# Hybrid DeltaNet and dilated-attention layer: first output factor turned before the step-48 scores, single blendings and stores moved by a third of a step, row splits and last loads re-placed

## The chip, the cores and the metric

The kernel runs on one core of one Trainium2 chip. The metric is the device time of one execution in microseconds, taken as the median over runs. Engines are named as in the profile: PE (TensorE), DVE (VectorE), ACT (ScalarE), POOL (GpSimd), SP (SyncE, which here only issues DMAs; ACT issues some too).

## The reference, cut to what matters

One layer on x of 2048 x 1024 float32. A combined projection feeds two mixers whose outputs are concatenated and projected back.

```python
h = rms_norm(x, norm_w)
proj = h @ w_in                                   # 1024 x 4104
qkv_dn, z_dn, b_dn, a_dn, qkv_att, gate_att = split(proj)
y_dn  = rms_norm(gated_delta_rule(silu(conv(qkv_dn)), ...)) * silu(z_dn)   # 2048 x 512
# attention, 8 heads of 64; q and k are RMS-normed
for window, dilation in ((128, 1), (512, 4), (2048, 16)):
    scores = q k^T + rel_bias, masked to the band; lse = logsumexp(scores)
    o = softmax(scores) v
o = sum over patterns of softmax(lse) * o
y_att = o * silu(gate_att)                                                  # 2048 x 512
out = x + concat(y_dn, y_att) @ w_out             # 1024 x 1024
```

## The kernel before, in words

Up to about 800 us it projects and runs the delta rule, whose result goes to DRAM as y_d. The rest, from line 838 on, is issued exactly in the order in which the Python code stands: a `Queue` class (line 99, which is why most rows show L99) ties every instruction of an engine to the one before it.

**Attention.** Pairs of heads are worked in 8 groups G[0] to G[7], each in 12 steps, so 96 steps; `step(t, gen, n)` issues one. A step runs what the table `at_step(t, third, ...)` has put at its three thirds and these parts: scores (PE `sc` into two PSUM buffers, DVE adds the bias and takes the minimum, `pr<-sc,bias`, shown as CUSTOM_DVE_ANT_0 in the profile and ISA in the order, then ACT's exponential `pr<-pr,ml`), on odd steps the values of two earlier steps (PE `pv`, ACT copy `op`), and the turning of the scores before (PE transposes `pt`, copied to `pT` by DVE and ACT). POOL spreads queries (`qz<-q`) and copies keys (`C<-K`).

**Fill.** Between these parts PE gets matmuls of another matrix product, `n` of them in the three thirds of a step: up to step 47 the attention projections (`pj`, 128x256; a norm needs the sums `ss`, which POOL finishes by an add and a power, and DVE then writes `t<-pj,ss` and so frees the `pj` buffer), from step 48 on the output projection (`po`, 128x512). The output projection is a list of jobs, one for 128 rows and one kind of factor: "dn" (from y_d, loaded as `yt`, turned by four PE transposes `po<-cs,yt`) or "att" (from mx_d, loaded as `mt`, no turning). `split` makes two parts of a factor, ACT's CAST `mh<-po` or `mh<-mt` and DVE's subtraction `mh<-po,mh`; the job's 24 or 18 matmuls follow, three for each 128 columns (high by high weights, high by low, low by high), so the third needs DVE's part. Step 48 took 1, 1 and 4 of the generator's items, of which the first two set up weights and the first factor; later steps take 4, 4 and 3 matmuls.

**After a group's scores.** Its softmax sums go out (`ml<-mr`) and back (`mm<-ml`, six loads, `sums_back` twice with three), are weighed on DVE (`M`, `e`, `lt`), written as F, and the group is blended in four quarters `qd`: `blend_load` (Fb, gt), `blend` (POOL, ending in `gt<-gt,Fb`), and `mixed` (the store mx_d<-gt), from which att jobs load.

**Weights.** The raw rows 4 to 7 of w_out are loaded during the first jobs (`raw_load`) and split by `wo_split` at the (job, matmul) pairs in `raws`: ACT `xh<-res` or `xh<-K`, DVE `xl<-res,xh`.

**Loads.** All loads here come from SP in written order. `load(upto)` issues the loads of the factors up to a job number; `yt` and `mt` have two buffers each, so a load waits until the factor two earlier is consumed. Buffers named `bias` (two, of another pool) hold the score biases and are not used after the last group's scores.

Of the kernel before, what the change touches and what calls it, by code (L numbers as in the profile page):

```python
# [8 lines left out]
F32 = mybir.dt.float32  # L9
# [7 lines left out]
P = 128  # L17
# [67 lines left out]
def hybrid(tc, xT, x, norm_w, w_in, conv_w, a_log, dt_bias, dn_norm_w, q_norm_w, k_norm_w,  # L85
# [23 lines left out]
    nc = tc.nc  # L109
# [13 lines left out]
    dma = nc.sync.dma_start  # L123
    adma = nc.scalar.dma_start
# [94 lines left out]
    nc = engines  # L219
    dma = nc.sync.dma_start  # L220
    adma = nc.scalar.dma_start
# [4 lines left out]
    for _ in range(14):  # L226
# [5 lines left out]
                                                        bufs=3 if b + g < 2 else 1) for n in ("wh", "wl"))  # L232
# [117 lines left out]
    for g, (tb, b, i) in enumerate(groups):  # L350
# [12 lines left out]
        k = g if tb == 0 else (g - 4) % 8  # L363
# [867 lines left out]
    def take(gen, n):  # L1231
        for _ in range(n):
            next(gen, None)
# [27 lines left out]
    def at_step(t, where, f, *args):  # L1261
        todo.setdefault((t, where), []).append((f, args))
# [3 lines left out]
    for i, g in enumerate(G):  # L1266
        b = 12 * i
        if i:
            at_step(*((b - 4, 1) if i < 4 else (b - 3, 0) if i == 4 else (b - 3, 2)), g["load"])
        at_step(b - (2 if i else 3), 1, g["queries"], 0)  # L1270
        for k in range(1, 6):
            at_step(b + 2 * k - 3, 0, g["queries"], k)
        at_step(b, 0, g["keys"], 1)
        at_step(b + 4, 0, g["keys"], 2)
        for j, t, where in (((0, -1, 0), (2, 1, 0), (4, 3, 0), (5, 4, 0), (6, 6, 0), (7, 7, 2), (8, 8, 0), (10, 10, 0))
                            if i < 4 else
                            ((0, 0, 0), (2, 1, 2), (4, 3, 2), (5, 4, 0), (6, 6, 0), (7, 7, 2), (8, 8, 0), (9, 9, 2),
                             (10, 10, 0), (11, 11, 2))):
            at_step(b + t, where, g["vload"], j)
        at_step(b + 12, 1, g["sums"])  # L1280
        at_step(b + 12, 2, g["sums_out"])
        if i < 7:
            at_step(b + 13, 2, g["sums_back"], 0, dma)
            at_step(b + 14, 0, g["sums_back"], 1, dma)
            at_step(b + 15, 1, g["weigh"])
            at_step(b + 15, 2, g["weigh2"])
            at_step(b + 16, 0, g["factors"])
            for qd in range(4):
                d = i < 6
                at_step(b + 16 + qd + d, 0 if d else 2, g["blend_load"], qd)  # L1290
                at_step(b + 17 + qd + d, 0 if d else 1, g["blend"], qd, nc.gpsimd)
                at_step(b + 19 + qd + d, 0 if d else 1, g["mixed"], qd)
                at_step(b + 20 + qd + 2 * d - (i == 6), 0 if i < 6 else 2, ready.add, (i // 4, i % 4, qd))
        else:
            at_step(b + 13, 0, g["sums_back"], 0, dma)
            at_step(b + 13, 1, g["sums_back"], 1, dma)

    def run(t, where):
        for f, args in todo.pop((t, where), ()):
# [2 lines left out]
    def step(t, gen, n):  # L1302
        run(t, 0)
        if 0 <= t < NST:
            G[t // 12]["scores"](t % 12)
        take(gen, n[0])
        run(t, 1)
        if t % 2 and 0 <= t - 3 < NST:
            G[(t - 3) // 12]["values"]((t - 3) % 12)
        if 0 <= t - 1 < NST:  # L1310
            G[(t - 1) // 12]["turned"]((t - 1) % 12)
        take(gen, n[1])
        run(t, 2)
        take(gen, n[2])
# [29 lines left out]
    def half_load(tt, kind, n):  # L1344
        if kind == "dn":
            t = wo.tile([P, 512], F32, name="yt", bufs=2)
            dma(t, y_d[tt * P:(tt + 1) * P, :])
        else:
            t = wo.tile([P, 512], F32, name="mt", bufs=2).rearrange("p (k c) -> p k c", k=4)
            dma(t[:, :n], mx_d[:n, :, tt * P:(tt + 1) * P].rearrange("k p c -> p k c"))  # L1350
        return t

# [30 lines left out]
    def out_fill():  # L1383
# [15 lines left out]
        def load(upto):  # L1399
            while n_loaded[0] <= min(upto, len(jobs) - 1):  # L1400
                tt, kind, n = jobs[n_loaded[0]][:3]
                if kind == "att" and not all((tt // 8, k, tt % 8 // 2) in ready for k in range(n)):
                    return
                loaded[n_loaded[0]] = half_load(tt, kind, n)
                n_loaded[0] += 1
# [20 lines left out]
        wo_tiles(1)  # L1426
        yield
        ops = split(0)
        load(2)
        yield  # L1430
        raws = {(0, 1): (raw_load, 0), (0, 2): (raw_load, 1), (0, 12): (raw_load, 2), (0, 22): (raw_load, 3)}
        for k, at_ in enumerate(((0, 20), (1, 8), (1, 20), (2, 8))):
            raws[at_] = (lambda k=k: wo_split(4 + k, RAW[k]),)
        store = None
        nth = -1
        for i, (tt, kind, n, mm, buf) in enumerate(jobs):
            if mm is None:
                continue
            nth += 1
            first, last = mm  # L1440
            todo_ = []
            while i + 1 + len(todo_) < len(jobs):
                todo_.append(i + 1 + len(todo_))
                if jobs[todo_[-1]][3]:
                    break
            if first:
                res = RES[tt] if kind == "att" else res_load(tt, x)
                po = [None, None]
            m = 0
            for b in range(2):  # L1450
                if first:
                    po[b] = psX.tile([P, 512], F32, name="po", bufs=3)
                for _ in products(po[b], ops, b, first, last):
                    m += 1
                    if (nth, m) in raws:
                        f, *args = raws.pop((nth, m))
                        f(*args)
                    if m >= 3 * n and m % 3 == 0 and todo_:
                        nxt = split(todo_.pop(0))
                    if nth in (18, 19, 20, 21, 23) and m == 3 * n + 8:  # L1460
                        k = min(nth - 18, 4)
                        RES[Q2[k]] = res_load(Q2[k], acc_d, K0[:, k * D:(k + 1) * D] if k < 2 else None)
                    if m >= 4:
                        load(i + 3 if nth < 24 else i + 5)
                    if m == 3 * n + 4 and store:
                        dma(*store)
                        store = None
                    yield
                if last:
                    cs_ = slice(b * 512, (b + 1) * 512)  # L1470
                    nc.vector.tensor_tensor(res[:, cs_], po[b], res[:, cs_], op=ALU.add)
            assert not todo_
            ops = nxt
            if last and not (kind == "att" and n == 3):
                store = ((out if kind == "att" else acc_d)[tt * P:(tt + 1) * P, :], res)

    gen = out_fill()
    q1 = {}
    RES = {}
    for t in range(48, NST + 2):  # L1480
        if t >= 92:
            psS[:] = [psT, "pt", 2]
        step(t, gen, {48: (1, 1, 4)}.get(t, (4, 4, 3)))
    g = G[7]
    take(gen, 18)
    g["weigh"]()
# [66 lines left out]
```

## Time and profile before

| | |
|---|---|
| median of 3 runs | 1397.85 us (1396.52 to 1399.55) |
| profiled execution, its own time | 1397.04 us |
| span of its profile | 1395.2 us |
| PE busy | 1362.5 us, 98% |
| PE weight loads | 1216.4 us, 87% |
| DVE, ACT, POOL busy | 855.7, 677.6, 486.2 us (61%, 49%, 35%) |
| granted PE clock, mean | 0.997 of full |

Busy times are sums over engines that work at once. A matmul's end is modelled, so the busy time of PE overlaps between neighbours; the start of one row against the start of the row before is the safer reading. The brackets in a timeline row give the idle time just before it and the engine whose signal ended it.

### The profile page before, as it was taken

How to read it: one execution, taken by the hardware profiler on the slowest of the kernel's cores; microseconds unless marked ns; L12 is line 12 of the kernel's file. 1: busy time of each engine (PE TensorE's matmuls, PEld its weight loads, DVE VectorE, ACT ScalarE, POOL GpSimd, SP SyncE). 2: the span in 40 equal slices, each digit the busy share in tenths (PEclk: the TensorE clock that was granted, in tenths of full speed). 3: DMA queues.
4: the chain of work that ended last, by engine and by line, in shares of the span. 5: the costliest groups of instructions: out<-in, count | busy, mean ns of one | idle time of the engine just before them, and what ended most of it. 6: DMA issues, size and time to landing. Idle time of an engine off the chain costs nothing.

```text
span 1395.2 us, 28823 instructions
## 1 busy us (share of the span) xinstructions
PE 1362.5 (98%) x10262; PEld 1216.4 (87%) x10262; DVE 855.7 (61%) x2724; ACT 677.6 (49%) x1930; POOL 486.2 (35%) x572
## 2 busy tenths in 40 slices
PE   8999999999999999999999899999999999999998
PEld 7998787778888789999999889999998788888877
DVE  7535667799742358777787564635454746556464
ACT  5644425572321334444444476666556555555520
POOL 3000000000752113442343523575757385654500
PEclk9999999999999999999999999999999999999999
DMA  6654536756547736557553455273647685665764
GB/s 189 184 109 85 109 69 143 159 125 118 102 105 136 201 96 153 158 155 185 138 151 83 103 135 138 69 196 98 161 129 220 177 266 144 211 176 166 204 187 145
DMA packets 301323, 205.01 MB, mean 147 GB/s; under 512 B 149323, under 2 KB 271067, under 8 KB 300668
## 3 DMA queue, kind: packets, MB, share of 16 engines
q1 hardware_dynamic: 231372, 171.11, 49.6%
q10 hardware_dynamic: 69808, 32.06, 8.4%
q8 instruction: 81, 1.33, 0.4%
q14 instruction: 62, 0.51, 0.1%
HBM read 142.61 MB, written 60.50 MB: 146 GB/s over the span
## 4 chain that ended last, share of the span: by engine, by line
PE 80%; DVE 7%; DMA 4%; ACT 3%; POOL 2%; issue 2%; SPq 1%; ACTq 0%; DVEq 0%; POOLq 0%
PE pj L99 16%; PE po L99 10%; PE pj L207 7%; PE pj L208 7%; PE pj L206 7%; PE sc L99 7%; PE pz L99 6%; PE pv L99 4%; PE pt L99 4%; PE SU L733 2%; PE C L727 2%; ACT pr L99 1%; POOL Fb L99 1%; PE A L665 1%; PE pm L99 1%
## 5 line engine op out<-in xcount | busy, mean ns | idle before, releaser
L99 ACT ACTIVATE pr<-pr,ml 128x192 f32<-128x192 f32 (+2 forms) x384 | 156.8, 410 | 160.8 <-DVE ml L99 155.9
L99 PE MATMUL pj<-wh,xh 128*128 128x256 f32 (+1 forms) x776 | 227.1, 293 | 3.6 <-DVE t L99 2.3
L99 PE MATMUL pj<-wh,xl 128*128 128x256 f32 (+1 forms) x776 | 224.6, 289 | 0.0
L99 PE MATMUL pj<-wl,xh 128*128 128x256 f32 (+1 forms) x776 | 224.3, 289 | 0.0
L208 PE MATMUL pj<-xh,wl 128*128 128x512 f32 x512 | 203.5, 397 | 0.7 <-DVE wl L192 0.7
L206 PE MATMUL pj<-xh,wh 128*128 128x512 f32 x512 | 202.6, 396 | 0.0
L207 PE MATMUL pj<-xl,wh 128*128 128x512 f32 x512 | 202.6, 396 | 0.0
L99 PE MATMUL po<-xh,mh 128*128 128x512 f32 x424 | 148.5, 413 | 5.3 <-ACT mh L99 4.2
L99 PEld LDWEIGHTS pj<-wh,xh 128*128 128x128 f32 x776 | 146.4, 189 | 5.0 <-DVE t L99 2.7
L99 DVE CUSTOM_DVE_ANT_0 pr<-sc,bias 128x192 f32<-128x192 f32 (+2 forms) x384 | 100.1, 308 | 77.6 <-PE sc L99 76.7
L99 PEld LDWEIGHTS pj<-wh,xl 128*128 128x128 f32 x776 | 146.5, 189 | 0.5 <-issue 0.3
L99 PEld LDWEIGHTS pj<-wl,xh 128*128 128x128 f32 x776 | 146.6, 189 | 0.1
L478 DVE SCALAR_TENSOR_TENSOR cy<-cu,cw,cy 128x512 f32<-128x512 f32 x144 | 112.1, 778 | 19.8 <-ACT cy L476 17.8
L208 PEld LDWEIGHTS pj<-xh,wl 128*128 128x128 f32 x512 | 96.2, 188 | 23.4 <-DVE wl L192 1.1
L207 PEld LDWEIGHTS pj<-xl,wh 128*128 128x128 f32 x512 | 96.2, 188 | 22.1
L206 PEld LDWEIGHTS pj<-xh,wh 128*128 128x128 f32 x512 | 96.3, 188 | 21.7
L99 POOL COPY qz<-q 64x512 f32<-64x512 f32 x96 | 95.8, 998 | 54.0 <-PE sc L99 43.9
L99 DVE COPY pT<-pt 64x128 f32<-64x128 f32 (+2 forms) x220 | 69.4, 323 | 62.6 <-PE pt L99 59.1
L99 PEld LDWEIGHTS po<-xh,mh 128*128 128x128 f32 x424 | 78.0, 189 | 19.4 <-ACT mh L99 4.8
L99 POOL TENSOR_TENSOR Fb<-Fb,op 128x256 f32<-128x256 f32 x84 | 71.6, 866 | 60.1 <-DMA Fb<-F 59.5
L543 POOL MEMSET inv<- 128x1024 f32 x1 | 1.0, 955 | 260.0 <-ACT wh L191 260.0
L99 PE MATMUL po<-xl,mh 128*128 128x512 f32 x212 | 86.9, 410 | 0.0
(369 smaller groups left out, 3066.3 us busy)
## 6 DMA issues: line engine op xcount, KB each, us to landing
wraw<-in_w_in SPq DMA_DIRECT2D x44, 512.0 KB, 7.2
cv<-cy ACTq DMA_DIRECT2D x48, 256.0 KB, 2.6
Fb<-F SPq DMA_DIRECT2D x64, 192.0 KB, 5.6
xr<-in_xT SPq DMA_DIRECT2D x32, 256.0 KB, 4.0
kT<-cv SPq DMA_DIRECT2D x32, 256.0 KB, 3.5
qk<-qs ACTq DMA_DIRECT2D x64, 128.0 KB, 4.0
res<-in_x SPq DMA_DIRECT2D x13, 512.0 KB, 5.5
V<-v_d SPq DMA_DIRECT2D x20, 256.0 KB, 4.1
```

Of the source, the lines that this page charges most:

```text
L99: i = f(*args, **kw)
L206: nc.tensor.matmul(ps, wh[:, k, c * P:(c + 1) * P], xh[tb][:, kt, :], start=kt == 0, stop=False)
L207: nc.tensor.matmul(ps, wh[:, k, c * P:(c + 1) * P], xl[tb][:, kt, :], start=False, stop=False)
L208: nc.tensor.matmul(ps, wl[:, k, c * P:(c + 1) * P], xh[tb][:, kt, :], start=False, stop=kt == KT - 1)
L478: nc.vector.scalar_tensor_tensor(y, u[:, i:i + 512], cw[:, ct, i:i + 1], y, op0=ALU.mult, op1=ALU.add)
L543: eng.memset(Tt, 0.0)
L665: nc.tensor.matmul(pq[:, u], kT[:, u].rearrange("p s i -> p (s i)"), qT[:, u].rearrange("p s i -> p (s i)"), start=True, stop=True)
L727: nc.tensor.matmul(pc[:, s_], g["WQ"][:, u, s_], S0[:, s_], start=True, stop=True)
L733: nc.tensor.matmul(su[:, s_], g["Ks"][:, u, s_], VN, start=True, stop=True)
```

## The change

Seven edits to the order; no arithmetic changes.

```diff
         at_step table, groups i < 6
-                at_step(b + 17 + qd + d, 0 if d else 1, g["blend"], qd, nc.gpsimd)
-                at_step(b + 19 + qd + d, 0 if d else 1, g["mixed"], qd)
+                    k = 3 * (b + 18 + qd) + (i == 1 and qd == 3)
+                    m = 3 * (b + 20 + qd) + 3 * (i == 2 and qd == 3)
+                    at_step(*divmod(k - 3, 3), g["blend_load"], qd)
+                    at_step(*divmod(k, 3), g["blend"], qd, nc.gpsimd)
+                    at_step(*divmod(m, 3), g["mixed"], qd)
         last group
-            at_step(b + 13, 1, g["sums_back"], 1, dma)
+            at_step(b + 13, 1, g["sums_back"], 1, adma)
 half_load
-            t = wo.tile([P, 512], F32, name="mt", bufs=2).rearrange("p (k c) -> p k c", k=4)
+            if tt in (8, 13):
+                t = at0.tile([P, 3, 192], F32, name="bias", bufs=2).rearrange("p a b -> p (a b)")[:, :512]
+            else:
+                t = wo.tile([P, 512], F32, name="mt", bufs=2)
+            t = t.rearrange("p (k c) -> p k c", k=4)
 out_fill
         ops = split(0)
-        load(2)
-        for k, at_ in enumerate(((0, 20), (1, 8), (1, 20), (2, 8))):
+        for k, at_ in enumerate(((0, 20), (1, 18), (2, 10), (3, 2))):
             raws[at_] = (lambda k=k: wo_split(4 + k, RAW[k]),)
-                        load(i + 3 if nth < 24 else i + 5)
+                        load(i + (2 if nth < 4 and m < 16 else 3 if nth < 20 else 4 if nth < 24 else 5))
 main
+    take(gen, 2)
     for t in range(48, NST + 2):
-        step(t, gen, {48: (1, 1, 4)}.get(t, (4, 4, 3)))
+        step(t, gen, (4, 3, 3) if 84 <= t < 91 else (4, 4, 3))
```

In words: (1) the last quarter's blending of group 1, with its load, is a third of a step later; on POOL this puts the add and the power on `ss` ahead of that blending, which is the only change of POOL's order. (2) The last mixed store of group 2 is a step later, on SP behind the first two `yt` loads. (3) The first factor is set up before step 48, whose thirds then hold 11 matmuls instead of 4; steps 84 to 90 hold 10 instead of 11, so the matmul counts agree again from step 91 on. (4) Factor loads look ahead two jobs at first, then 3, 4 and 5, where it was 3 and 5. (5) The row splits of w_out come after 20, 42, 58 and 74 matmuls instead of 20, 32, 44 and 56. (6) The `mt` tiles of row blocks 8 and 13 take the `bias` buffers, so the later `mt` loads wait for an earlier consumer. (7) Three of the last group's six `mm` loads are issued by ACT instead of SP.

The first place is the boundary at step 48, on PE (`pj` is the last projection fill, `sc` the scores of step 48, `po<-xh` and `po<-xl` the first output job). Before:

```order
L99 MATMUL pj<-wl,xh_9197 128x256
L99 MATMUL pj<-wh,xl_9198 128x256
L99 MATMUL sc<-K_8200,qz_8743 128x192 x4
L99 MATMUL po<-cs,ml 96x128
L99 MATMUL pt<-cs,pr 128x128 x2
L99 MATMUL po<-cs,yt 128x128 x4
L99 MATMUL po<-xh_12395,mh 128x512
```

And now:

```order
L99 MATMUL pj<-wl,xh_9197 128x256
L99 MATMUL pj<-wh,xl_9198 128x256
L99 MATMUL po<-cs,yt 128x128 x4
L99 MATMUL sc<-K_8200,qz_8743 128x192 x4
L99 MATMUL po<-xh_12395,mh 128x512
L99 MATMUL po<-xl_12396,mh 128x512
L99 MATMUL po<-xh_12395,mh 128x512 x2
L99 MATMUL po<-cs,ml 96x128
L99 MATMUL pt<-cs,pr 128x128 x2
```

The four transposes moved ahead of the scores, and four matmuls of the first job stand between the scores and the next turning. On ACT at the same place the CAST of that factor stood behind the exponentials of step 48:

```order
L99 ACTIVATE t_12640<-pj,rstd 128x256 x2
L99 DMA v_d<-t_12640 128x2x256
L99 ACTIVATE pr,ml<-pr,ml 128x192 x4
L99 COPY pT_8751<-pt 64x128 x2
L99 CAST mh<-po 128x512
```

and now stands ahead of them:

```order
L99 ACTIVATE t_12639<-pj,rstd 128x256 x2
L99 DMA v_d<-t_12639 128x2x256
L99 CAST mh<-po 128x512
L99 ACTIVATE pr,ml<-pr,ml 128x192 x4
L99 COPY pT_8751<-pt 64x128 x2
```

Only the CAST moved (DVE's subtraction moved likewise, ahead of its four `pr` of step 48).

The second place is DVE around the weighing of group 3, which ends with the bias-and-minimum rows (ISA) of step 52. Before:

```order
L99 TENSOR_TENSOR xl_12682<-res,xh_12681 128x1024
L99 TENSOR_TENSOR lt<-e,mm 32x64
L99 TENSOR_TENSOR lp<-e,mm 32x64
...
L99 RECIPROCAL lt<-lt 32x64
L99 TENSOR_TENSOR e<-e,lt 32x192
L99 TENSOR_TENSOR mh<-po,mh 128x512
L99 TENSOR_TENSOR res<-po,res 128x512
L99 ISA pr,ml<-sc,bias 128x192
```

And now:

```order
L99 TENSOR_TENSOR lt<-e,mm 32x64
L99 TENSOR_TENSOR lp<-e,mm 32x64
...
L99 RECIPROCAL lt<-lt 32x64
L99 TENSOR_TENSOR e<-e,lt 32x192
L99 TENSOR_TENSOR xl_12662<-res,xh_12661 128x1024
L99 ISA pr,ml<-sc,bias 128x192
```

The row split now follows the weighing, and the factor's subtraction and the residual's addition are no longer between it and the ISA rows.

The third place is ACT in the last group, where the two-part casts of the last att factors stand (`mh<-mt` twice for row blocks 14 and 15, `C<-mt` for block 9, `mh<-bias` for block 13). Before:

```order
L99 CAST K_15654<-mt 128x384
L99 CAST mh<-mt 128x384
L99 COPY op_15665<-pv 128x512
L99 CAST C_15790<-mt 128x384
L99 CAST mh<-mt 128x384
L99 ACTIVATE e<-e 32x192
```

And now:

```order
L99 CAST K_15656<-mt 128x384
L99 CAST mh<-bias 128x384
L99 DMA mm<-ml_94 16x2x64
L99 DMA mm<-ml_94 16x8x16
L99 DMA mm<-ml_94 16x32x4
L99 COPY op_15667<-pv 128x512
L99 CAST C_15792<-mt 128x384
L99 CAST mh<-mt 128x384
L99 ACTIVATE e<-e 32x192
```

Three DMA issues were added to ACT's order ahead of the last `op` copy and two casts; on SP the same three are gone, and the loads of blocks 9 and 14 now go out together ahead of `ml<-mr`, where 13 and 9 did.

## Rows read from the trace of the kernel before

**Rows 1.** The page, part 1: busy us of each engine, share of the span, instructions.

```profile
PE 1362.5 (98%) x10262; PEld 1216.4 (87%) x10262; DVE 855.7 (61%) x2724; ACT 677.6 (49%) x1930; POOL 486.2 (35%) x572
```

**Rows 2.** Table of windows: start:end and length, busy us of each engine with its instructions, granted PE clock, DMA share, GB/s.

```profile
1066.00:1077.00 11.00, 7.97 (x38) 6.75 (x37) 6.09 (x22) 6.14 (x22) 4.84 (x4) 0.84 0.71 223
1116.00:1329.00 213.00, 213.00 (x1670) 184.01 (x1669) 118.25 (x495) 122.27 (x462) 127.54 (x133) 1.00 0.68 197
```

**Rows 3.** Waits of PE from 838 us to the end: who waited for whom, us in total, times, longest.

```profile
PE po L99 <- ACT mh L99: 4.2, 2, 2.5
PE pj L99 <- DVE t L99: 2.3, 1, 2.3
PE pt L99 <- ACT pT L99: 1.8, 1, 1.8
```

**Rows 4.** Timelines of POOL, DVE and PE, 983 to 993 us: start, duration, engine, instruction, idle before and its releaser.

```profile
985.19 1.57 POOL L99 TENSOR_TENSOR Fb<-Fb,op 128x256 f32<-128x256 f32 x2
...
990.00 0.20 POOL L99 TENSOR_TENSOR ss<-ss,e 128x8 f32<-128x8 f32 x1
990.27 1.65 POOL L99 TENSOR_TENSOR ss<-ss,mhalf 128x8 f32<-128x8 f32 x1
...
983.37 0.69 DVE L99 TENSOR_REDUCE ss<-t 128x8 f32<-128x512 f32 x1 [1.55 <-ACT t L99]
...
991.95 0.69 DVE L99 TENSOR_TENSOR t<-pj,ss 128x512 f32<-128x512 f32 x1 [4.14 <-POOL ss L99]
...
990.13 0.28 PE L99 MATMUL pj<-wh,xl 128*128 128x256 f32 x1
992.70 0.39 PE L99 MATMUL pj<-wh,xh 128*128 128x256 f32 x1 [2.29 <-DVE t L99]
```

**Rows 5.** Timelines of PE, DVE, ACT, SP and POOL around step 48, 1062 to 1074 us.

```profile
1066.76 1.46 PE L99 MATMUL sc<-K,qz 128*128 128x192 f32 x8
...
1069.02 0.33 PE L99 MATMUL pt<-cs,pr 128*128 128x128 f32 x1 [0.58 <-DVE pT L99]
1069.18 0.60 PE L99 MATMUL po<-cs,yt 128*128 128x128 f32 x4
1072.24 0.50 PE L99 MATMUL po<-xh,mh 128*128 128x512 f32 x1 [2.45 <-ACT mh L99]
...
1073.71 2.76 PE L99 MATMUL sc<-K,qz 128*128 128x192 f32 x8
...
1066.52 1.81 DVE L99 SCALAR_TENSOR_TENSOR xl<-wraw,dnw,xh 128x1024 fp32r<-128x1024 f32 x1 [2.11 <-ACT xh L99]
...
1068.26 0.37 ACTq L99 DMA_DIRECT2D v_d<-t  x1
...
1071.61 0.58 ACT L99 CAST mh<-po 128x512 fp32r<-128x512 f32 x1
...
1063.14 0.80 SPq L99 DMA_DIRECT2D yt<-y_d  x2
...
1063.32 3.93 POOL L99 COPY C<-K 128x2048 f32<-128x2048 f32 x1 [0.66 <-DVE xl L99]
```

**Rows 6.** Timelines of DVE and PE, 1092 to 1114 us.

```profile
1093.76 1.23 DVE L99 TENSOR_TENSOR xl<-res,xh 128x1024 fp32r<-128x1024 f32 x1 [1.75 <-ACT xh L99]
...
1096.97 0.67 DVE L99 TENSOR_TENSOR mh<-po,mh 128x512 fp32r<-128x512 f32 x1
...
1098.16 0.33 DVE L99 CUSTOM_DVE_ANT_0 pr<-sc,bias 128x192 f32<-128x192 f32 x1
...
1092.82 1.46 PE L99 MATMUL sc<-C,qz 128*128 128x192 f32 x8
...
1098.84 1.57 PE L99 MATMUL sc<-C,qz 128*128 128x192 f32 x8 [1.39 <-DVE ml L99]
...
1113.21 0.50 PE L99 MATMUL po<-xh,mh 128*128 128x512 f32 x1 [0.82 <-DVE mh L99]
```

**Rows 7.** Timelines of SP, ACT, DVE and PE in the last group's end, 1331 to 1347 us.

```profile
1334.31 3.21 SPq L99 DMA_DIRECT2D mm<-ml  x6
1337.62 0.97 SPq L99 DMA_DIRECT2D mt<-mx_d  x2
...
1340.20 0.51 ACT L99 CAST mh<-mt 128x384 fp32r<-128x384 f32 x1 [5.33 <-DMA mt<-mx_d]
...
1331.12 0.56 DVE L99 TENSOR_TENSOR K<-mt,K 128x384 fp32r<-128x384 f32 x1 [1.05 <-ACT K L99]
...
1340.77 0.50 PE L99 MATMUL po<-xh,mh 128*128 128x512 f32 x1 [1.73 <-ACT mh L99]
...
1346.07 0.72 PE L99 MATMUL po<-xh,mh 128*128 128x512 f32 x2 [0.33 <-DVE mh L99]
```

**Rows 8.** What bounds the unknown costs: the issue of two stores on ACT's queue at 1032 us and ACT's next work (timeline), POOL's key copy at 1078 us (timeline), and two kinds of DMA with KB each and median us from issue to landing (the DMA list of 1050 to 1080 us).

```profile
1032.53 1.58 ACTq L99 DMA_DIRECT2D qk<-qs  x2
1034.16 0.35 ACT L99 ACTIVATE pr<-pr,ml 128x64 f32<-128x64 f32 x1 [5.41 <-DVE ml L99]
...
1078.85 3.75 POOL L99 COPY C<-K 128x2048 f32<-128x2048 f32 x1
...
yt<-y_d SPq DMA_DIRECT2D x3, 256.0 KB, 3.0
...
bias<-bs_d SPq DMA_DIRECT2D x2, 144.0 KB, 8.8
```

More of the change, by code (lines that the diff above doesn't have):

```diff
@@ L1288, in hybrid @@
             for qd in range(4):
-                d = i < 6
-                at_step(b + 16 + qd + d, 0 if d else 2, g["blend_load"], qd)
-                at_step(b + 17 + qd + d, 0 if d else 1, g["blend"], qd, nc.gpsimd)
-                at_step(b + 19 + qd + d, 0 if d else 1, g["mixed"], qd)
-                at_step(b + 20 + qd + 2 * d - (i == 6), 0 if i < 6 else 2, ready.add, (i // 4, i % 4, qd))
+                if i < 6:
+                    k = 3 * (b + 18 + qd) + (i == 1 and qd == 3)
[3 more added lines that the diff above has]
+                    at_step(*divmod(m, 3), g["mixed"], qd)
+                    at_step(*divmod(k + 12, 3), ready.add, (i // 4, i % 4, qd))
+                else:
+                    at_step(b + 16 + qd, 2, g["blend_load"], qd)
+                    at_step(b + 17 + qd, 1, g["blend"], qd, nc.gpsimd)
+                    at_step(b + 19 + qd, 1, g["mixed"], qd)
+                    at_step(b + 19 + qd, 2, ready.add, (i // 4, i % 4, qd))
         else:
             at_step(b + 13, 0, g["sums_back"], 0, dma)
-            at_step(b + 13, 1, g["sums_back"], 1, dma)
+            at_step(b + 13, 1, g["sums_back"], 1, adma)
     def run(t, where):
@@ L1348, in half_load @@
         else:
-            t = wo.tile([P, 512], F32, name="mt", bufs=2).rearrange("p (k c) -> p k c", k=4)
+            if tt in (8, 13):
+                t = at0.tile([P, 3, 192], F32, name="bias", bufs=2).rearrange("p a b -> p (a b)")[:, :512]
+            else:
+                t = wo.tile([P, 512], F32, name="mt", bufs=2)
+            t = t.rearrange("p (k c) -> p k c", k=4)
             dma(t[:, :n], mx_d[:n, :, tt * P:(tt + 1) * P].rearrange("k p c -> p k c"))
```

## The prediction

> **What bounds the kernel now.** I read the engines' shares first: PE is busy 1362.5 us of a span of 1395.2 [rows 1], so no engine but PE matters unless PE waits for it. Then the table of windows: between 1116 and 1329 us PE is busy 213.00 of 213.00 us, while around step 48 it has 7.97 of 11.00 and a granted clock of 0.84 [rows 2]. So a change of order can win only in single holes. The list of what PE waits for after 838 us shows how few there are: the largest are ACT's `mh`, twice, DVE's norm `t` once, ACT's `pT` once [rows 3]. The timelines around each give the place and the late instruction [rows 4 to 7]. The change takes away no matmul, so the sum is: which holes close, and what opens.
>
> I cost a hole from start to start. At 990.13 a 128x256 matmul starts, the next at 992.70, where its neighbours follow after about 0.12: 2.45 lost, of which the bracket prints 2.29 [rows 4]. So I add 0.16 to a bracket; that is a choice, and without it the sum is 1.1 smaller.
>
> **Part 1, POOL (blending of group 1).** DVE's sum `ss` is done at 984.06, but POOL starts a blending at 985.19 and gets to the power on `ss` only at 990.27, which lasts 1.65; DVE's norm starts at 991.95 and PE, out of `pj` buffers, waits until 992.70 [rows 4]. Now the add and the power come first. The two take 1.92 (990.00 to 990.27 + 1.65), so the norm can start near 987.1 instead of 991.95. PE asks for the buffer at 990.25, 3 us later. Gain **2.45**. The blending ends 1.92 later, at 991.9, and the query copies behind it on POOL start when they started before, so they cost nothing. Its loads now stand behind two V loads on SP; if they came more than 1.9 us late, the copies would too.
>
> **Parts 2 to 4, the boundary at step 48.** Now PE loses here 0.58 + 0.16 at 1069.02 (scores not copied yet by DVE) and 2.45 + 0.16 at 1072.24, where the first output matmul waits for ACT's CAST at 1071.61; the CAST stands behind four exponentials whose scores were themselves just made [rows 5]. Right after, the clock falls to its lower level: the scores at 1073.71 take 2.76 where the same eight take 1.46 at 1092.82 [rows 5, 6]. The window's mean of 0.84 means 0.32 of 11.00 us at 1.2 instead of 2.4 GHz, 3.5 us, of which half is lost: 1.76 [rows 2]. Together 0.74 + 2.61 + 1.76 = 5.11.
>
> After: PE turns the factor at 1066.76, when the old scores began, and does the scores behind it. ACT is busy until 1068.26 + 0.37 = 1068.63 and then does the CAST, which takes 0.58: ready near 1069.23. PE has the transposes (at most 0.60) and scores (at most 1.46) until 1068.4 to 1068.8 [rows 5]; I take 1068.4, so it waits **0.85**. DVE's subtraction, 0.67 [rows 6], is ready near 1069.95, where the third matmul comes. Eleven matmuls instead of four then hide the copies for the next turning, so the 0.74 is gone too. The clock: the 2.29 of idle time at 992.70 was not followed by a fall, by the list of matmuls behind it at the usual 0.12 spacing, and 1.73 at 1340.77 neither, so I take 0.85 as too short [rows 4, 7]. Gain 5.11 − 0.85 = **4.26**. The cover is the `yt` load: it was issued at 1063.14 [rows 5] and was not needed until 1069.18; now it is needed at 1066.76. With the 3.0 that such a load takes [rows 8] it is there by 1066.1, if it is issued no later than before (it has one transfer less ahead of it, so I take the same time); each us that it is later costs a us, since the scores stand behind the transposes. The moved store of group 2 goes behind this load on SP; its reader, a job load of mx_d, is many steps off.
>
> The clock is the one point where a rule weighs in. The Trainium skill, "TensorE: Matmul & The Clock Gate", section "Part 1: The HAM clock gate", says that the gate has only two rates and sets them by how busy the array has been lately. Its two levels agree with the 2.76 against 1.46. By that rule alone a fall need not be tied to one idle time: if the wait for the CAST met it again, the sum would be 1.76 smaller, which is worked out above and is a rival below.
>
> **Part 5, row splits.** At 1098.84 the scores of step 53 wait, 1.39 + 0.16 = **1.55**, for DVE's rows of step 52, which begin at 1098.16 though their scores were started at 1092.82. DVE spent the time on a split at 1093.76 (after 1.75 idle, waiting for ACT's `xh`), the weighing, a subtraction at 1096.97 and an addition [rows 6]. Now the weighing runs in that idle time, the split follows it, and the subtraction and addition (1098.16 − 1096.97 = 1.19) are behind. 1.75 + 1.19 = 2.94 against 1.55 needed: the hole closes. At 1113.21 a job waits 0.82 + 0.16 = **0.98** for DVE's subtraction [rows 6]; jobs are now seven matmuls further against the steps, and ACT's CAST there comes ahead of a step's exponentials, so this closes too.
>
> Against this part speaks a rule on ports. The split at 1066.52 took 1.81 while POOL copied keys until 1067.25; the one at 1093.76, with POOL idle, took 1.23 [rows 5, 6]. So a split that meets a key copy lasts 0.58 longer at least, and if it meets the start of one (3.75 long [rows 8]) up to 3.75. The first split moves from 1086.77 to about 1079, by my placing beside the copy of step 50. The Trainium skill, "SBUF — State Buffer", section "SBUF: two separate sides", says why: a DVE operation with two SBUF inputs and a GpSimd operation lock each other out for a whole instruction. By the row the split ends 0.6 later, which the scores of step 51, two steps' matmuls behind, don't need (I estimate 1.4 of slack, from some 80 rows of matmuls placed one behind the other). By the rule the split ends at worst 3.75 later and costs 3.75 − 1.4 = 2.3. I take the row, since the copy begins first.
>
> **Parts 6 and 7, the end.** At 1340.77 PE waits 1.73 + 0.16 = 1.89 for ACT's CAST of row block 14, ACT 5.33 for its load, and SP issued that load at 1337.62 behind six `mm` issues of 3.21 us [rows 7]. At 1346.07 another 0.33 + 0.16 = 0.49 go. Now that load needs only block 10's buffer, free at 1331.12 + 0.56 = 1331.68, and stands ahead of `mm`: 6 us earlier. ACT must first issue three `mm` loads (half of 3.21, 1.6) which wait for `ml` to land, near 1334.3: then 1335.9, the `op` copy, block 9's CAST and block 14's, each 0.5 to 0.6: ready at about 1337.5. PE asks at 1340.77 − 1.89 = 1338.88. Gain 1.89, and as DVE's weighing then starts 0.4 earlier against PE, 0.4 of the 0.49: **2.29**.
>
> **Unchanged.** ACT's `pT` at 1037 (1.8 [rows 3]) stays: ACT was held until 1034.16 by stores issued at 1032.53 [rows 8], and nothing there moves. Steps 84 to 90 give back the seven matmuls; the end after PE's last matmul is the same.
>
> **Sum.** 2.45 + 4.26 + 1.55 + 0.98 + 2.29 = 11.53. The profiled run took 1397.04 (span 1395.2 and 1.84 around it): 1385.5. The median is 0.81 above that run, so **1386.3**.
>
> **The rivals.**
> - The boundary keeps half: the clock falls again (1.76), or `yt` lands late behind the 1 MB key load that it now follows. At the longest row here, 8.8 from issue [rows 8], it lands at 1071.9, 5.2 late: 1386.3 + 1.8 to 5.2, say 1389.5. For it: the load has only 0.7 of slack. Against: DMA was able to land it by 1066.1 in the same neighbourhood.
> - DVE is late in steps 49 to 57, because a split meets POOL or the weighing moves less: 1.5 to 2.5 of part 5 stay: 1388.3.
> - The end gives nothing: ACT's DMA issues hold it. Two stores on ACT's queue at 1032.53 kept ACT from its next work for 5.41 [rows 8]. If the three `mm` issues end 3 us later than I have, block 14's CAST is at 1340.5 as before: 1388.6.
> - Slower: the transposes wait for `yt` on PE with the scores queued behind. The price is one for one, and the point at which the whole 11.5 is used up is a landing 11.5 us late, near 1078; slower by over 0.2%, 2.8 us (about what a measurement here can tell from no change), beyond 1081, 18 us after issue, twice the longest row.
> - No change to be seen: several holes reopen one step on, since how close DVE and ACT run ahead of PE between 1116 and 1329 is not to be seen where PE never waits [rows 2]: 1396.
>
> **How the numbers follow.** Chances: forecast 0.56 (1385 to 1388), boundary 0.11, DVE 0.12, end 0.12, no change 0.05, slower 0.04. Faster 0.91, same 0.05, slower 0.04. The three middle cases are worth 2 to 3.5 each, and two could meet: the range goes up to 1391. Down, the bracket's 0.16 and the 0.85 wait bound it, with medians that scatter by 1.5: 1384.
>
> **What would show it.** After: POOL's power on `ss` ahead of the last blending and no row of over 0.3 idle at 990 to 993; first `po<-xh,mh` about 2 us after the transposes with under 1 us of idle and clock 1.00 in the next 11 us; no `sc<-DVE ml` wait near step 53; ACT's CAST of block 14 without a wait for DMA. The forecast is wrong if new brackets appear on PE between 1066 and 1120, or if those named shrink without the time.

## The result and the profile after

The changed kernel takes 1386.76 us in the median (1385.32 to 1388.93, 4 runs) where the kernel before, beside it, takes 1398.70: a ratio of 0.9914 with a 95% interval of 0.9889 to 0.9939. The profiled execution took 1385.32 with a span of 1383.5, 11.7 less than the one before.

PE does the same work with fewer holes. Part 1 of the page of after, which answers to [rows 1], and the waits of PE after 838 us, which answer to [rows 3] (who waited for whom, us, times, longest):

```profile
PE 1360.6 (98%) x10262; PEld 1215.8 (88%) x10262; DVE 857.3 (62%) x2724; ACT 675.8 (49%) x1930; POOL 484.7 (35%) x572
...
PE pt L99 <- ACT pT L99: 0.8, 1, 0.8
PE po L99 <- ACT mh L99: 0.7, 1, 0.7
PE pt L99 <- DVE pT L99: 0.7, 1, 0.7
```

The wait for DVE's norm is gone, that for ACT's `mh` fell from 4.2 to 0.7. The longest that is left, 1.3 for DVE's `ml` at 846 us, stands ahead of all that was changed and is the same in both; the rest are 0.4 or less each. **The first hole**, POOL and DVE (start, us, engine), to be read beside [rows 4]:

```profile
984.47 1.65 POOL L99 TENSOR_TENSOR ss<-ss,mhalf 128x8 f32<-128x8 f32 x1
986.09 1.56 POOL L99 TENSOR_TENSOR Fb<-Fb,op 128x256 f32<-128x256 f32 x2
...
986.97 0.67 DVE L99 TENSOR_TENSOR t<-pj,ss 128x512 f32<-128x512 f32 x1
```

The power now stands ahead of the blending, and DVE's norm runs at 986.97 without a bracket. **The boundary at step 48**, PE, ACT and SP, then the window, beside [rows 5] and [rows 2]:

```profile
1062.47 0.60 PE L99 MATMUL po<-cs,yt 128*128 128x128 f32 x4
1062.90 1.47 PE L99 MATMUL sc<-K,qz 128*128 128x192 f32 x8
1065.08 0.50 PE L99 MATMUL po<-xh,mh 128*128 128x512 f32 x1 [0.71 <-ACT mh L99]
...
1063.97 0.37 ACTq L99 DMA_DIRECT2D v_d<-t  x1
1064.44 0.58 ACT L99 CAST mh<-po 128x512 fp32r<-128x512 f32 x1 [0.49 <-PE sc L99]
...
1059.02 1.00 SPq L99 DMA_DIRECT2D yt<-y_d  x2
...
1062.00:1073.00 11.00, 10.29 (x71) 8.45 (x70) 7.44 (x25) 7.81 (x27) 7.28 (x6) 1.00 0.67 215
```

PE waits once, 0.71, the scores take 1.47 and the granted clock stays at 1.00. The bracket of the CAST names PE's scores, but these are only the last signal before it: the CAST starts 0.10 after ACT's own issue of `v_d` ends (1063.97 + 0.37 = 1064.34), as forecast, and in the run with a late factor below, where that issue is long done, it starts 2.5 us before the scores end. **The last group**, beside [rows 7]: SP, ACT and PE.

```profile
1318.65 3.84 SPq L99 DMA_DIRECT2D mt<-mx_d  x2
...
1324.91 1.88 SPq L99 DMA_DIRECT2D mm<-ml  x3
...
1327.75 0.51 ACT L99 CAST mh<-mt 128x384 fp32r<-128x384 f32 x1
...
1334.35 0.72 PE L99 MATMUL po<-xh,mh 128*128 128x512 f32 x2 [0.33 <-DVE mh L99]
```

The loads of blocks 9 and 14 go out ahead of the `mm` loads, and block 14's CAST waits for none; the second, small hole of [rows 7] is still there, and just as long. Two holes are new or left over. At 1206 us POOL's key copy and DVE's subtraction start 0.02 us apart, DVE takes 4.24 us for what takes it 0.69 elsewhere, and PE waits; at 1091 us DVE is a little late again, after 1.11 spent waiting for a residual load:

```profile
1200.80 3.71 POOL L99 COPY C<-K 128x2048 f32<-128x2048 f32 x1
...
1200.82 4.24 DVE L99 TENSOR_TENSOR mh<-mt,mh 128x512 fp32r<-128x512 f32 x1 [1.54 <-ACT mh L99]
...
1206.06 0.55 PE L99 MATMUL pt<-cs,pr 128*128 128x128 f32 x3 [0.70 <-DVE pT L99]
...
1084.38 0.69 DVE L99 TENSOR_TENSOR res<-po,res 128x512 f32<-128x512 f32 x1 [1.11 <-DMA res<-in_x]
...
1090.88 1.57 PE L99 MATMUL sc<-C,qz 128*128 128x192 f32 x8 [0.34 <-DVE ml L99]
```

PE issues the same 10262 matmuls in both, so the start of the matmul with the same number can be subtracted. That is how gains are given below: it is worked out from the traces, and it counts what lies between two places, holes and clock together. Against the kernel before it is used only up to step 48 and from step 91 on, since between them the same number is not the same matmul. By it the changed kernel's profiled execution was ahead by 0.8 at 975 us, before anything that was changed; by 3.3 after the first hole; 4.35 at 1060; 9.6 at 1320; 11.7 at the end.

### The profile page after: what moved, and what is told of

Same layout as the page of the kernel before. It is cut to its first block, busy times and chain, and to the rows that moved or that the text cites. A ratio compares the mean times of both kernels' runs of the same rounds, so it can differ in the third digit from the quotient of the medians.

```text
span 1383.5 us, 28812 instructions
## 1 busy us (share of the span) xinstructions
PE 1360.6 (98%) x10262; PEld 1215.8 (88%) x10262; DVE 857.3 (62%) x2724; ACT 675.8 (49%) x1930; POOL 484.7 (35%) x572
## 4 chain that ended last, share of the span: by engine, by line
PE 85%; DVE 6%; DMA 4%; ACT 3%; issue 2%; ACTq 0%; SPq 0%; POOL 0%; DVEq 0%
PE pj L99 18%; PE po L99 10%; PE sc L99 8%; PE pj L208 7%; PE pj L207 7%; PE pj L206 7%; PE pz L99 6%; PE pv L99 5%; PE pt L99 4%; PE SU L733 2%; PE C L727 2%; PE pm L99 1%; PE A L665 1%; PE A L688 1%; PE A L701 1%
```

## The experiments

### Each part alone on the kernel before

**Part 1 alone.**

```diff
+                late = i == 1 and qd == 3
-                at_step(b + 16 + qd + d, 0 if d else 2, g["blend_load"], qd)
-                at_step(b + 17 + qd + d, 0 if d else 1, g["blend"], qd, nc.gpsimd)
+                at_step(b + 16 + qd + d, 1 if late else 0 if d else 2, g["blend_load"], qd)
+                at_step(b + 17 + qd + d, 1 if late else 0 if d else 1, g["blend"], qd, nc.gpsimd)
```

> The kernel before with part 1 alone (blending and load of the last quarter of group 1 a third of a step later). Theory: the wait of PE for DVE's norm at 990 to 993 us (2.29 in brackets, 2.45 start to start) disappears and nothing else does, so the time falls by 2.4 us to about 0.998 of before. Rival: the shorter wait of PE for ACT's pT near 1033 us in the changed kernel (0.75 in brackets against 1.77) also comes from part 1, through the moved loads on SP; then that bracket is about 0.75 here too and the time falls by 3.4 us. If it is again near 1.8, or somewhere else, it is the pace of the DMAs in that execution.

1394.22 us against 1398.48, ratio 0.9975 (0.9964 to 0.9985). The hole is gone and nothing else is: PE's wait for ACT's `pT` near 1033 is 1.5 here, so its shortening to 0.75 is not this part's. The 3.5 us of the ratio (4.3 between the medians) are more than the hole's 2.45; the next runs say why.

**Part 3 alone.**

```diff
+    take(gen, 2)
-        step(t, gen, {48: (1, 1, 4)}.get(t, (4, 4, 3)))
+        step(t, gen, (4, 3, 3) if 84 <= t < 91 else (4, 4, 3))
```

> The kernel before with part 3 alone (first factor turned ahead of the scores of step 48, that step with 11 matmuls, steps 84 to 90 with 10); splits, look-ahead of loads and the rest as before. Theory: at step 48 PE waits 0.7 to 1.0 us once for ACT's CAST instead of 0.58 and 2.45, and the granted clock of the 11 us around stays 1.00 instead of 0.84: 4.1 us gained there. The row splits stay where they were in matmuls, but the seven matmuls move them against the steps, so the waits at 1098.8 (1.39) and 1113.2 (0.82) should change: by the theory the second goes with part 3 and the first needs part 5. Time 4 to 5 us less, 0.9965 of before. Rival: the clock falls here too, because it does not hang on the length of the one wait; then about 2.3 us.

1396.99, ratio 0.998 (0.9967 to 0.9992): 2.8 us by the ratio and 1.5 between the medians, where 4 to 5 were expected. At step 48 it did what it should, one wait of 0.7 and a granted clock of 1.00 in the window. But six holes stand behind it up to 1216 us. PE's waits in this run:

```profile
PE sc L99 <- DVE ml L99: 1.6, 3, 0.8
...
PE pt L99 <- DVE lt L99: 0.5, 1, 0.5
```

DVE is late three times for the scores and once behind the weighing (`lt`). So part 3 alone doesn't keep its gain; other parts let it stay. Which ones, the later runs show in part: the two holes at 1094 and 1098 us come back when part 5 is undone (below), so the splits make them. The three from 1131 to 1142 us, 2.1 us by the matmul starts against the changed kernel, don't come back with it. There DVE waited 2.20 for a residual load and PE 0.34 for a key load, both issued late by SP; that points to part 4, the look-ahead of loads, but no run takes part 4, or part 2, by itself, so this is not shown. And the run shows something else. Behind the first hole, which this kernel still has, the clock fell, as in every later run that has that hole, but not in the profile of before. The window of 991 to 999 us of before, and of the runs of parts 3, 6 and 7 alone, in this order (clock is the third figure from the end):

```profile
991.00:999.00 8.00, 6.30 (x58) 6.00 (x59) 3.21 (x17) 4.22 (x16) 6.63 (x8) 1.00 0.77 173
...
991.00:999.00 8.00, 6.72 (x50) 6.33 (x51) 2.53 (x12) 3.72 (x13) 6.63 (x8) 0.79 0.91 195
...
991.00:999.00 8.00, 5.81 (x43) 5.21 (x43) 2.52 (x12) 3.71 (x13) 6.62 (x8) 0.79 0.93 196
...
991.00:999.00 8.00, 5.80 (x42) 5.20 (x42) 2.41 (x12) 3.54 (x14) 6.55 (x10) 0.79 0.94 202
```

The three agree: 0.79 each, and by the matmul starts 1.4 to 1.6 us go on top of the wait. The one profile of before was the exception.

**Part 6 alone, and part 7 alone.**

```diff
             # part 6, half_load
-            t = wo.tile([P, 512], F32, name="mt", bufs=2).rearrange("p (k c) -> p k c", k=4)
+            if tt in (8, 13):
+                t = at0.tile([P, 3, 192], F32, name="bias", bufs=2).rearrange("p a b -> p (a b)")[:, :512]
+            else:
+                t = wo.tile([P, 512], F32, name="mt", bufs=2)
             # part 7, last group
-            at_step(b + 13, 1, g["sums_back"], 1, dma)
+            at_step(b + 13, 1, g["sums_back"], 1, adma)
```

> The kernel before with part 6 alone (mt tiles of row blocks 8 and 13 in the bias buffers); all mm loads stay on SP. Theory: since the load of block 14 goes by the ring of two mt buffers, only the load of block 13 goes out earlier and that of 14 keeps its place behind the six mm loads unless the look-ahead is changed as well; ACT still waits some 5 us for it and PE 1.7: no gain, within 0.3 us. Rival: the buffers alone make the gain of the last group, 1.9 to 2.1 us.

> The kernel before with part 7 alone (three of the six mm loads of the last group issued by ACT). Theory: the load of block 14 leaves SP earlier by the three issues, half of 3.21 us = 1.6 us, so ACT's CAST of block 14 is 1.6 us earlier and PE waits 0.1 to 0.3 instead of 1.73: 1.5 us gained. Rival: ACT is held by its own issues, which wait for ml to land, and its casts of blocks 9 and 14 are late instead: no gain, or a loss of up to 1 us.

Part 6: 1396.81, ratio 0.9987 (0.9978 to 0.9997); part 7: 1397.27, 0.9991 (0.9975 to 1.0008), not to be told from no change by time. The traces tell more. SP, ACT and PE of part 6 alone, then of part 7 alone:

```profile
1334.48 4.07 SPq L99 DMA_DIRECT2D mm<-ml  x6
1338.65 0.96 SPq L99 DMA_DIRECT2D mt<-mx_d  x2
...
1341.23 0.51 ACT L99 CAST mh<-mt 128x384 fp32r<-128x384 f32 x1 [4.61 <-DMA mt<-mx_d]
...
1341.80 0.50 PE L99 MATMUL po<-xh,mh 128*128 128x512 f32 x1 [1.01 <-ACT mh L99]
```

```profile
1337.28 2.03 SPq L99 DMA_DIRECT2D mm<-ml  x3
1339.47 1.89 SPq L99 DMA_DIRECT2D mt<-mx_d  x2
...
1337.33 2.00 ACTq L99 DMA_DIRECT2D mm<-ml  x3
1339.37 0.59 ACT L99 COPY op<-pv 128x512 f32<-128x512 f32 x1 [4.50 <-DMA mm<-ml]
...
1341.89 0.51 ACT L99 CAST mh<-mt 128x384 fp32r<-128x384 f32 x1 [1.52 <-DMA mt<-mx_d]
...
1342.46 0.50 PE L99 MATMUL po<-xh,mh 128*128 128x512 f32 x1 [0.45 <-ACT mh L99]
```

With part 6 alone the load still goes out behind the six issues, and PE waits 1.01 where it was 1.73; I had expected no gain. (In the three profiles with neither part 6 nor part 7 this wait is 1.57 to 1.95.) With part 7 alone it still stands behind three, and PE waits 0.45. Three issues took 2.0 us on each queue here, where half of the 3.21 for six on one [rows 7] was expected. Over all runs the times scatter: three on each of two queues took 1.4 to 2.0 in nine profiles, six on SP alone 3.0 to 4.1 in five, so half is about right in the mean.

### The changed kernel with a part undone

**Part 5 undone** (row splits after 20, 32, 44, 56 again).

```diff
-        for k, at_ in enumerate(((0, 20), (1, 18), (2, 10), (3, 2))):
+        for k, at_ in enumerate(((0, 20), (1, 8), (1, 20), (2, 8))):
```

> The changed kernel with part 5 undone (row splits after 20, 32, 44 and 56 matmuls again). Theory: the splits put DVE behind in steps 50 to 57, as in the kernel before and in the run of part 3 alone: waits of PE for DVE's ml or pT of 1 to 2.5 us in sum between 1080 and 1110 us against 0.5 now, so 0.5 to 2 us slower than the changed kernel. Rival: the holes there come from the jobs' phase or the late residual load and not from the splits: the same holes as in the changed kernel, within 0.3 us.

1388.81, ratio 0.9938 (0.9918 to 0.9958). PE's holes between 1080 and 1110 us:

```profile
1091.01 1.21 PE L99 MATMUL pt<-cs,pr 128*128 128x128 f32 x6 [0.51 <-DVE lt L99]
...
1094.67 1.57 PE L99 MATMUL sc<-C,qz 128*128 128x192 f32 x8 [0.83 <-DVE ml L99]
```

1.34 in brackets against 0.34, 1.6 us between 1085 and 1092 us by the matmul starts: so much the placing of the splits is worth here. The time alone doesn't show it (the intervals of the ratios overlap). The `lt` wait of the run of part 3 alone is theirs too.

**Part 7 undone** (all `mm` loads on SP again).

```diff
-            at_step(b + 13, 1, g["sums_back"], 1, adma)
+            at_step(b + 13, 1, g["sums_back"], 1, dma)
```

> The changed kernel with part 7 undone (all six mm loads of the last group on SP again). Theory: the load of block 14 now stands ahead of them in SP's order because of the look-ahead and the bias buffers, so ACT's issues are not needed: no wait of ACT for the load, PE's wait of 0.33 near 1334 us the same or 0.2 less, time within 0.3 us of the changed kernel. Rival: the six issues on SP make the weighing or block 15 late: 0.5 to 1.5 us slower, as PE's wait for DVE's mh near 1334 us.

1388.74, ratio 0.9929 (0.9911 to 0.9947), which overlaps the changed kernel's. In the last group nothing changes: block 14's load is ahead of the six issues anyway, and PE's small hole is again there:

```profile
1330.25 0.69 DVE L99 TENSOR_TENSOR res<-po,res 128x512 f32<-128x512 f32 x1 [0.88 <-PE po L99]
1330.85 0.25 DVE L99 TENSOR_TENSOR M<-mm 32x64 f32<-32x64 f32 x1
...
1335.11 0.73 PE L99 MATMUL po<-xh,mh 128*128 128x512 f32 x2 [0.37 <-DVE mh L99]
```

DVE's weighing (from M) comes behind an addition that waits for PE's own last matmul of the job before; from there to PE's matmul it is 4.26 us, with 4.25 before and 4.24 in the changed kernel, whatever ACT and SP do. So the gain of the last group comes from the load's place. By the code that is due to the buffers and the look-ahead together (part 6 alone left the load behind the six issues); the look-ahead wasn't undone by itself. Once these are there, ACT's issues add nothing that the trace shows. (The median is 2 us above that of the run with two further moves below, which ran beside it; the trace gives no place for so much, and this stays open.)

**Part 1 undone.**

```diff
-                    k = 3 * (b + 18 + qd) + (i == 1 and qd == 3)
+                    k = 3 * (b + 18 + qd)
```

> The changed kernel with part 1 undone. Theory: PE waits 2.2 for DVE's norm again near 989 us, and in most executions the granted clock falls behind it, as it did in the runs of parts 3, 6 and 7 alone (0.57 to 0.80 in the 4 us after) and not in the first profile of the kernel before: 3.6 us slower than the changed kernel. Rival: only the wait itself, 2.4 us.

> The changed kernel as it is, for a second profile and for a time next to the two below. Theory: of what PE lost in its first profile, the wait of 0.70 for DVE's pT near 1206 us and the short wait for ACT's pT near 1033 us (0.75) are not marks of the change: DVE's subtraction and POOL's key copy start there within 0.02 us of each other and whichever is first goes, and the stores on ACT's queue wait for w_out loads. The second profile then shows about 1.7 near 1033 and either 0.70 or nothing near 1206. The marks of the change are the same: no wait near 987, 0.71 at step 48, none for block 14. Rival: both are fixed by the order and come back within 0.2 us.

Run together, with the changed kernel once more: 1390.59, ratio 0.9933 (0.9918 to 0.9948), against 1386.01, 0.9909 (0.9892 to 0.9926): 3.4 us slower by the ratios, though their intervals just overlap. The window behind the hole reads

```profile
991.00:999.00 8.00, 5.80 (x43) 5.21 (x43) 2.42 (x12) 3.94 (x16) 6.55 (x10) 0.79 0.96 200
```

and by the matmul starts 4.0 us go between 975 and 1000 us of the changed kernel's time: 2.4 of wait, 1.6 of clock. The second profile of the changed kernel has the same marks (no wait near 987, 0.70 at step 48, none of block 14's CAST) and no hole at 1206, as expected, but its wait for `pT` near 1033 is 0.66, not 1.7: that expectation missed.

### A late factor

The first two raw loads of w_out ahead of the `yt` loads:

```diff
+    for k in range(2):
+        dma(RAW[k], w_out[(4 + k) * P:(5 + k) * P, :])
     loaded = {i: half_load(Q2[i], "dn", 4) for i in range(2)}
```

> The changed kernel with the first two raw loads of w_out (512 KB each) issued ahead of the two yt loads, so that the first factor comes late. Nothing else moves. Theory: PE waits before the first yt transposes for as long as the load is late, by the transfers ahead of it 2 to 5 us, with the scores of step 48 behind it; a wait of over 2 us there is followed by a fall of the granted clock, another 1.2 to 1.8 us: 3.5 to 6.5 us slower than the changed kernel, 5 to 8 us faster than before. Rival: the load still lands in time because the DMA has room: no difference.

1392.57, ratio 0.9963 (0.9945 to 0.998). SP, ACT, PE and a window of PE's clock:

```profile
1061.51 3.98 SPq L99 DMA_DIRECT2D res<-in_w_out  x2
1065.54 0.90 SPq L99 DMA_DIRECT2D yt<-y_d  x2
...
1071.03 0.58 ACT L99 CAST mh<-po 128x512 fp32r<-128x512 f32 x1 [4.59 <-PE po L99]
...
1069.88 1.12 PE L99 MATMUL po<-cs,yt 128*128 128x128 f32 x4 [4.76 <-DMA yt<-y_d]
1070.78 2.77 PE L99 MATMUL sc<-K,qz 128*128 128x192 f32 x8
...
1070.00:1074.00 4.00, 4.00 (x14) 3.90 (x15) 1.72 (x8) 1.58 (x6) 0.00 (x0) 0.50 1.04 365
```

The load is issued 3.7 us later than in the changed kernel (1065.54, less the 2.8 by which this execution is behind there already, against 1059.02) and has a megabyte ahead of it. PE stands for 4.76 us with the scores behind the transposes, and the granted clock is at half when it goes on: the scores take 2.77 again. By the matmul starts 6.2 us are lost between 1060 and 1075 us against the changed kernel: 4.9 of wait and 2.3 of clock, less 1.0 for the changed kernel's own wait, which falls away. The median is 5.9 above that of the run with two further moves below, which ran beside it.

### Further moves

First two (the step's matmuls put the subtraction ahead of the key copy; three `mm` loads go behind the residual load), then a third (w_out rows 24 matmuls later):

```diff
-        step(t, gen, (4, 3, 3) if 84 <= t < 91 else (4, 4, 3))
+        step(t, gen, {72: (4, 4, 4), 73: (3, 4, 3)}.get(t, (4, 3, 3) if 84 <= t < 91 else (4, 4, 3)))
-            at_step(b + 14, 0, g["sums_back"], 1, dma)
+            at_step(b + 14, i == 3, g["sums_back"], 1, dma)
-                    if o8 == 1:
+                    if o8 == 2:
                         rs = [w_out_load(k) for k in range(3)]
```

> The changed kernel with two more moves. First, steps 72 and 73 take (4, 4, 4) and (3, 4, 3) matmuls instead of (4, 4, 3) twice, so that DVE's subtraction of a factor comes ahead of POOL's key copy, with which it started at once (4.24 us instead of 0.69, and PE waits 0.70 for DVE's pT near 1206 us). Second, the second three mm loads of group 3 go out a third of a step later, behind a residual load, for which DVE waits 1.11 near 1084 us (PE waits 0.34 for DVE's ml near 1091 us). Theory: the subtraction takes about 0.7 there and the hole of 0.86 start to start is gone; DVE's wait for the residual load is gone and with it the 0.5 start to start: 1.3 us faster than the changed kernel. Rival to the first: it is the moved phase of jobs and not the meeting of DVE and POOL; then the subtraction still takes over 2 us. Rival to the second: the weighing is bound by its mm loads and not by the residual load; then the wait near 1091 us stays.

1386.72, ratio 0.9916 (0.9899 to 0.9933), no gain that time can tell. The holes at 1091 and 1206 are gone. But both are gone in other runs without the moves too. At 1091 the runs with part 1 undone, with part 7 undone and with the late factor have none; there DVE waits 0.33 or less for the residual load, in the three profiles with the hole 1.1 to 1.3. So the load makes the hole, and how late it is differs by execution. At 1206, with part 7 undone, DVE and POOL start at the same hundredth, and this time DVE isn't held up:

```profile
1202.49 0.69 DVE L99 TENSOR_TENSOR mh<-mt,mh 128x512 fp32r<-128x512 f32 x1 [1.53 <-ACT mh L99]
...
1202.49 4.30 POOL L99 COPY C<-K 128x2048 f32<-128x2048 f32 x1
```

The copy takes 0.6 longer instead, and PE doesn't wait for it.

> The changed kernel with DVE's subtraction of step 73 ahead of POOL's key copy (as in the run with both moves) and with the first three w_out rows loaded 24 matmuls later, behind the next quarter's Fb and gt loads, so that the two stores on ACT's queue near 1028 us do not wait behind 1.5 MB of loads. Theory: ACT issues these stores within 1 us of the query product and PE's wait for ACT's pT (1.5 to 1.8 in most runs) is gone; the splits of w_out that follow have 4 us of slack: 1.9 us faster than the changed kernel, and up to 2.8 where that one loses at the key copy. Rival: the loads meet other stores or the key load of group 4 and the wait moves a few us on: no gain.

The third move with the first: 1385.13, ratio 0.9895 (0.9879 to 0.9911). ACT's two stores go out right behind their product, and PE has no wait for `pT` there:

```profile
1026.55 0.67 ACT L99 ACTIVATE qs<-pm,qw 128x512 f32<-128x512 f32 x1
1027.25 0.82 ACTq L99 DMA_DIRECT2D qk<-qs  x2
```

> The changed kernel with all three further moves: the subtraction of step 73 ahead of POOL's key copy, the first three w_out rows loaded 24 matmuls later, and the second three mm loads of group 3 a third of a step later, behind the residual load. Theory: no wait of PE for ACT's pT near 1030 us, none for DVE's pT near 1200, none for DVE's ml near 1091: 2.4 us less than the changed kernel's median, a ratio of 0.989 to before. Rival: the wait near 1091 us stays (0.4 to 0.5), because the later w_out loads or the weighing itself hold DVE: a ratio of 0.9895 as without that move.

All three: 1383.91 (1383.26 to 1386.48), ratio 0.9898 (0.988 to 0.9916). PE's waits after 838 us are down to

```profile
PE pj L99 <- DVE ml L99: 1.3, 1, 1.3
PE po L99 <- ACT mh L99: 0.7, 1, 0.7
PE po L99 <- DVE mh L99: 0.4, 1, 0.4
PE pv L99 <- DVE pT L99: 0.3, 1, 0.3
```

The last line of that list, 0.2, is left out. The trace has fewer holes than the changed kernel's and the median is 2 to 3 us lower, but the two didn't run side by side and the intervals of the ratios overlap: it is faster than the kernel before, and likely, not certainly, faster than the changed one.

## Why the prediction was right

The forecast, 1386.3 with faster at 0.91, holds. Its steps, one by one:

- **Part 1, 2.45.** The hole closed: 2.55 came in the two profiles. The norm starts at 986.97; this execution is 0.8 ahead, so that is 987.75 in the time of before, for the forecast 987.1. Two copies of `pT` on DVE stand ahead of it, which I had left out, and PE's slack of 3 us covers them. But in most executions the part was worth more, 3.4 to 4.0 us by the ratios and the matmul starts: I took one profile, in which the clock did not fall behind the hole, as the rule. Four of the five profiles with this hole show the fall. The sentence that 0.85 was too short for a fall came out right. Of its two grounds, that 1.73 at the end was not followed by one held in the other profiles too, with waits of 1.57 and 1.95 there; that 2.29 was not was the chance of one profile. The rule of the Trainium skill that I set beside it ("TensorE: Matmul & The Clock Gate", section "Part 1: The HAM clock gate": the rate follows how busy the array has been lately) was the better guide, as it ties the fall to no single wait. The runs agree in so far as waits of one length were followed by a fall in four profiles and by none in the fifth.
- **The boundary, 4.26.** Measured by what is left after the other terms between 1060 and 1320 us (9.6 − 4.35 = 5.2, less 1.05 and 0.99, plus 0.86 for the hole at 1206): about 4.1. The wait is 0.71 in brackets, 1.0 start to start, for 0.85, and it came about as worked out, ACT's CAST behind its own issue. The `yt` load came in time. What I did not see is that the gain needs other parts as a cover: alone, part 3 brought 0.2% for the 0.35% expected. Part 5 is shown to be one of them; for the rest part 4 is likely and not tested.
- **Part 5, 1.55 and 0.98.** The second closed. Of the first a part was left, since DVE waited for a residual load that I had not followed: 1.05 for 1.55, and the sign "no `sc<-DVE ml` wait near step 53" failed by 0.34 (0.53 in the second profile). The slack for the first split held: it met the key copy, took 2.13 (2.12 in the run with the late factor), 0.9 more than the 1.23 of [rows 6] where I had 0.6, and no one waited.
- **The end, 2.29.** 2.1 came (9.6 to 11.7): 1.89 at the matmul that had waited and 0.24 in those right behind it, which I had not costed. The further 0.4 did not: the step that failed is that "DVE's weighing then starts 0.4 earlier against PE". It starts behind an addition that waits for PE, and the hole is 0.33 as before.
- **What was not in the sum.** Plus: 0.8 before 975 us, which is the same code in both, and 1.0 at the `pT` wait near 1033, of the same order in both. Minus: 0.86 at 1206. Together about +0.9, and the terms above came to 0.7 less than the 11.53: that the sum met the 11.7 of the profiled runs so closely is in part luck. Both profiles of the changed kernel have the short `pT` wait (0.75, 0.66) and the run with part 1 undone as well (0.75), five other runs with the same order up to there have 1.5 to 1.8; what sets it is not settled, beyond that ACT's stores there wait behind w_out loads, since moving these ends it.

The rivals: none decided. The boundary lost only where the load was issued late, and then 6.2, not the whole gain; the end was not held by ACT's issues, though ACT stood 4.94 before its `op` copy with them and 2.38 without; DVE's lateness took 0.5 of the 1.5 to 2.5 given.

## What to carry to other kernels

In a kernel whose bound engine is 98% busy, list its holes start to start and ask of each which order of issue makes it; the sum of those that a change closes was a good forecast here, but a change that moves the phase of a fill has to be followed through every later meeting of two engines, because alone it may give its gain back a few steps on. One profile is not enough to say that a wait brings no fall of the clock or that a near tie between two engines goes one way: where two starts lie within some hundredths, count both outcomes. A wait of an engine behind its own DMA issues, and a load behind small loads on one queue, are worth a look wherever the load's order can be changed instead of its queue.

## What the runs showed of the hardware

- **A tie for a port is decided by hundredths of a microsecond.** DVE's subtraction of 128x512 with two SBUF operands took 4.26, 4.24 and 4.05 in the three executions in which POOL's copy of 128x2048 started 0.01, 0.02 and 0.24 earlier, and 0.69 in four in which both starts read alike, the copy then taking 4.30 for 3.71. That agrees with what the Trainium skill says ("SBUF — State Buffer", section "SBUF: two separate sides": whichever starts first holds the shared ports for the whole instruction), and I had put the price at 0.6 by a row in which the copy was nearly over. The trace of before had a better one: there the same subtraction meets the copy (1209.84, 3.73) in its middle and ends 0.55 behind it.

```profile
1211.83 2.29 DVE L99 TENSOR_TENSOR mh<-mt,mh 128x512 fp32r<-128x512 f32 x1 [0.85 <-ACT mh L99]
```

A subtraction with one operand in PSUM took its usual 0.69 in the middle of a copy (1081.42 in the trace of before, the copy of [rows 8]). In the three runs with the moved subtraction the two don't meet.
- **The same wait is not followed by a fall of the clock in each execution**: behind waits of 2.2 to 2.3 the granted clock of 991 to 999 us was 1.00 once and 0.79 four times, the lower level each time for the same part of the window.
- **Issuing on two queues at once** took 1.4 to 2.0 us for three loads on each in nine profiles, against 3.0 to 4.1 for six on one in five: about half. One pair of runs, 2.0 and 3.21, would have said otherwise.
